# Layer 0's modulation as fp32 products on four 32-column tiles, and a pooling mixer with channels on partitions

## The chip, the cores and the metric

The kernel runs on one core of a Trainium2 chip. The metric is device time: three runs took 1964.33, 1965.14 and 1966.70 us, median 1965.14 us. Work is spread over TensorE (matmuls and transposes into PSUM), VectorE, ScalarE, GpSimd, and DMA transfers issued from SyncE. In the rows PE is TensorE, PEld its weight loads, DVE VectorE, ACT ScalarE, POOL GpSimd, SP SyncE.

## The reference

A two-layer decoder trunk on 256 tokens of width 2048, batch one, fp32. Layer 0 mixes tokens by causal pooling, layer 1 by latent attention (which the change leaves alone); both have a SwiGLU FFN of width 5632. Each sub-layer is modulated by a conditioning vector `c`. What matters here:

```python
sc = jax.nn.silu(c)
shift_m, scale_m, gate_m, shift_f, scale_f, gate_f = jnp.split(sc @ mod_w[i] + mod_b[i], 6, axis=-1)
h = modulate(rmsnorm(x, norm_mix[i]), shift_m, scale_m)       # h * (1 + scale) + shift
y = pool_mixer(h, pool_w[i], pool_scale[i])                   # layer 0
x = x + gate_m[:, None, :] * y
h = modulate(rmsnorm(x, norm_ffn[i]), shift_f, scale_f)
x = x + gate_f[:, None, :] * swiglu(h, ffn_gate[i], ffn_up[i], ffn_down[i])
```

`pool_mixer` takes, in four groups of 512 channels, the causal mean over 2, 4, 8 or 16 tokens less the value itself, multiplies each group by a 512x512 matrix and scales the channels by `pool_scale`. `mod_w[0]` alone is 2048 x 12288 fp32, 100 MB; a sixth of it (2048 x 2048, a "part") is 16.8 MB.

## The kernel before

Weights arrive as units of 1 MiB (128 x 2048 fp32, or 512 x 512) in a ring of six buffers, `raw`. For the large projections each unit is split exactly into two fp32r halves (ScalarE copies the upper half, L368, VectorE subtracts it, L370) and multiplied in three combinations: 24 matmuls of 512 columns a unit (L392). The program calls everything ahead of the first of these the front; it makes layer 0's mixer and the first quarter of the FFN's hidden state.

The modulation of the front is four groups of units: shift (16 units), scale (16), gate (16) and the first 512 columns of the FFN's shift and scale ("block 0", 8 units). In `Part.add` (L183) VectorE multiplies a unit by 128 values of silu(c), one for each partition, and adds it to an accumulator 128 x 2048; at the end TensorE sums over partitions with a vector of ones (L275). For the gate, `SharedPart` gives five of the 16 row tiles to TensorE as fp32 matmuls with the value of c repeated over 128 columns (L200), and adds VectorE's accumulator the same way (L199). Block 0 (`BlockPart`, L219 to L247) is divided too: seven row tiles by TensorE with one column of weights (L230), nine by VectorE (L233).

The mixer holds tokens on partitions at its ends and channels on partitions in the middle: band matrices times the normed stream (L726, L727), scale and shift per channel (L797 on ScalarE, L799 on VectorE), the 512x512 products (L784) with tokens on partitions again, `pool_scale` (L791), the gate and the residual add (L525, L526), squares for the norm (L410), and for each quarter of the hidden state a scaling by token (L432 or L434), eight transposes (L444) and the modulation (L458 to L460).

Two things set the order. Inside `tc.manual_schedule()` instructions stand as they are written; elsewhere a scheduler orders each engine's queue by priority. `pump(n)` emits the next n units of a list of background work, which is how gate and block 0 are interleaved with the mixer here, and blocks 1 to 3 of the FFN's shift and scale with the start of the FFN. In that start (`start_ffn`), twelve projections go through quarter after quarter of the hidden state, and the next quarter's scaling, transposes and modulation are emitted between units. The residual stream `x` is written aside to DRAM at the FFN's fifth chunk (`stream_aside`).

## Time and profile before

| | us |
|---|---|
| median of three runs | 1965.14 |
| span of the profiled execution, first to last instruction | 1962.3 |
| TensorE, first fp32r product of the FFN starts at | 184.32 |
| TensorE busy after 184 us, of 1778.3 | 1751.0 |
| TensorE busy in the whole span | 1853.0 |
| VectorE busy in the whole span | 1546.4 |

The profile lists one execution of 1962.3 us; the 2.8 us up to the median lie outside its first and last instruction. Up to 184 us the DMA engines move weights for the front and TensorE works in bursts; from there on TensorE is busy nearly without a break. A busy share is that of a stretch, so the front has to be read by itself.

### The profile page before, as it was taken

What the parts mean: (1) busy time and instruction counts of PE and PEld (TensorE: products, weight loads), DVE (VectorE), ACT (ScalarE), POOL (GpSimd) and SP (SyncE); (2) the same over time, 40 slices, a digit from 0 to 9 for tenths busy, and PEclk for the clock granted to TensorE, in tenths of its full rate; (3) what the DMA queues carried; (4) which work ended last, traced back from release to release, by engine and by line L of the source; (5) the groups of instructions that cost most, each with busy time, mean ns of one, the idle gap of its engine ahead of it and who ended that gap; (6) DMA issues with size and microseconds to landing.
All of it is one profiled execution on the core that took longest, in us unless ns stands there. A gap on an engine that the chain in (4) does not pass through costs nothing. (4 is left out here: it accounts for less than half of the span.)

```text
span 1962.3 us, 21516 instructions
## 1 busy us (share of the span) xinstructions
PE 1853.0 (94%) x8485; PEld 1520.7 (77%) x8485; DVE 1546.4 (79%) x1312; ACT 850.0 (43%) x939; POOL 35.9 (2%) x33
## 2 busy tenths in 40 slices
...
GB/s 377 408 378 365 379 321 305 310 350 327 313 329 302 332 325 345 338 333 284 307 311 304 228 295 142 360 303 325 297 293 260 225 229 257 235 209 186 195 219 70
DMA packets 225184, 572.66 MB, mean 292 GB/s; under 512 B 11958, under 2 KB 16286, under 8 KB 203442
## 3 DMA queue, kind: packets, MB, share of 16 engines
...
## 5 line engine op out<-in xcount | busy, mean ns | idle before, releaser
L392 PE MATMUL ps<-hl,act 128*128 128x512 f32 x7008 | 1609.5, 391 | 4.7 <-ACT act L459 2.2
L392 PEld LDWEIGHTS ps<-hl,act 128*128 128x128 f32 x7008 | 1315.1, 188 | 279.3 <-ACT act L459 4.4
L370 DVE TENSOR_TENSOR hl<-raw,hl 128x2048 fp32r<-128x2048 f32 x296 | 676.2, 2289 | 239.9 <-ACT hl L368 236.1
L368 ACT ACTIVATE hl<-raw 128x2048 fp32r<-128x2048 f32 x296 | 566.4, 1919 | 608.7 <-PE ps L392 542.1
L183 DVE SCALAR_TENSOR_TENSOR acc<-raw,s_col,acc 128x2048 f32<-128x2048 f32 x155 | 364.0, 2348 | 4.2 <-DMA raw<-in_mod_w_dram 1.6
L233 DVE SCALAR_TENSOR_TENSOR acc<-raw,s_col,acc 128x1024 f32<-128x1024 f32 x121 | 155.0, 1281 | 8.7 <-DMA raw<-in_mod_w_dram 7.2
L556 DVE TENSOR_TENSOR act<-ps,act 128x512 f32<-128x512 f32 x96 | 64.6, 687 | 14.1 <-PE ps L392 13.7
L275 PE MATMUL ps<-ones,acc 128*128 128x1 f32 x64 | 13.9, 352 | 62.8 <-DVE acc L183 39.9
L410 ACT ACTIVATE junk<-x 128x512 bf16<-128x512 f32 x40 | 25.2, 630 | 89.6 <-DVE x L526 44.1
L275 PEld LDWEIGHTS ps<-ones,acc 128*128 128x128 f32 x64 | 13.8, 332 | 64.5 <-DVE acc L183 41.4
L590 ACT ACTIVATE act<-ps 128x512 fp32r<-128x512 f32 x44 | 23.8, 596 | 61.5 <-PE ps L587 53.4
L625 DVE TENSOR_TENSOR x<-ps,x 128x512 f32<-128x512 f32 x32 | 22.1, 691 | 35.4 <-PE ps L392 35.4
L458 ACT ACTIVATE t2k<-ps,cols 128x256 f32<-128x256 f32 x64 | 33.2, 567 | 21.6 <-PE ps L444 17.0
L634 ACT ACTIVATE t2k<-ps 128x512 f32<-128x512 f32 x24 | 14.2, 593 | 64.2 <-PE ps L392 64.2
L918 PE MATMUL ps<-act,hl 128*128 128x256 f32 x128 | 37.2, 291 | 0.6 <-DVE hl L370 0.6
L919 PE MATMUL ps<-act,hl 128*128 128x256 f32 x128 | 36.7, 287 | 0.0
L920 PE MATMUL ps<-act,hl 128*128 128x256 f32 x128 | 36.1, 286 | 0.0
L591 DVE TENSOR_TENSOR act<-ps,act 128x512 fp32r<-128x512 f32 x44 | 28.2, 685 | 8.1 <-ACT act L590 8.0
L638 DVE TENSOR_TENSOR t2k<-ps,t2k 128x512 f32<-128x512 f32 x24 | 16.6, 690 | 21.3 <-PE ps L392 21.3
L444 PE MATMUL ps<-con,t2k 128*128 128x128 f32 x144 | 22.5, 306 | 11.2 <-DVE t2k L432 8.1
L784 PE MATMUL ps<-act,act 128*128 128x512 f32 x64 | 30.7, 644 | 0.9 <-issue 0.9
L554 ACT ACTIVATE act<-ps 128x512 f32<-128x512 f32 x32 | 19.1, 598 | 28.3 <-PE ps L392 28.1
...
## 6 DMA issues: line engine op xcount, KB each, us to landing
raw<-in_mod_w_dram SPq DMA_DIRECT2D x128, 1024.0 KB
...
raw<-in_mod_w_dram SPq DMA_DIRECT2D x128, 512.0 KB
...
```

What stands on the lines that cost most here:

```text
L183: dve.scalar_tensor_tensor(out=self.acc, in0=r, scalar=s_col[:, self.kt:self.kt + 1], in1=self.acc, op0=ALU.mult, op1=ALU.add)
L233: dve.scalar_tensor_tensor(out=self.acc, in0=r[:, k], scalar=s_, in1=self.acc, op0=ALU.mult, op1=ALU.add)
L368: hi_ins = act.activation(hi, r, AF.Copy)
L370: lo_ins = dve.tensor_tensor(out=lo, in0=r, in1=hi.bitcast(F32), op=ALU.subtract)
L392: pe.matmul(banks[tok], lhsT=t_[:, i, k, tok * P:(tok + 1) * P], rhs=w[:, k, :], start=first and n < len(part), stop=last and n >= len(ord ...
L458: act.activation(full, pts[k // 2][:, k % 2, :], AF.Identity, scale=scale, bias=bias)
L556: dve.tensor_tensor(out=part, in0=banks[tok], in1=part, op=ALU.add)
L591: dve.tensor_tensor(out=m[:, 1, :, ts_], in0=v, in1=m[:, 0, :, ts_].bitcast(F32), op=ALU.subtract)
L784: pe.matmul(pt, lhsT=pooled[g // 2][:, g % 2, k, tok * P:(tok + 1) * P], rhs=wp[g][:, k, :], start=k == 0, stop=k == KL - 1)
L918: pe.matmul(pt[:, h, :], lhsT=wl(h0 + h, k), rhs=t_[:, 0, k, :], start=k == 0, stop=False)
L919: pe.matmul(pt[:, h, :], lhsT=wh(h0 + h, k), rhs=t_[:, 0, k, :], start=False, stop=False)
L920: pe.matmul(pt[:, h, :], lhsT=wh(h0 + h, k), rhs=t_[:, 1, k, :], start=False, stop=k == KL - 1)
```

## The change

The layer 0 modulation leaves VectorE. A class `Strips` takes every unit of shift, scale, gate and block 0. The unit's 2048 columns are four strips of 512; each is an fp32 matmul of its own whose weights are 32 columns wide (silu(c) in the first, zeros in the others), and the four write rows 0, 32, 64 and 96 of one PSUM bank. The built program gives them the tile size 128 x 32 and the tile positions 0, 32, 64 and 96. After 16 units (8 for block 0) ScalarE copies the bank, and four small matmuls with a selecting matrix turn the four rows into columns with channels on partitions, to which VectorE adds the bias.

The mixer keeps channels on partitions to its end. The residual stream is transposed at the start (`xT`, which takes the memory of `x`), products give channels by tokens, and gate, pool scale and residual add are one VectorE instruction for each 128 channels. The sum of squares is taken by TensorE (32 matmuls of one column). The reciprocal root, one value for each token, is spread over partitions: a diagonal matrix times ones. The hidden state needs one multiplication with that row and no transposes. The stream is transposed back for the copy in DRAM, which is now written while the FFN's start is in its second quarter.

All of the front stands in a fixed order, given by a table: after unit n of the 56, these functions. The first five units and both halves of x are requested at once.

```diff
+    crow = t2k([KD, P])
+    vrows = t2k([V_END, P])
+    brows = t2k([5 * KD, P])
+
+    def load_x(tok):
+        sync.dma_start(xn[tok], a["x"][0, tok * P:(tok + 1) * P, :])
...
+    def load_ahead():
+        kt = len(ahead)
+        ahead.append(raw_t([P, 1, NSTRIP, CH]))
+        sync.dma_start(ahead[kt].rearrange("p k i n -> p (k i n)"), a["mod_w"][0, kt * P:(kt + 1) * P, :D])
...
+    load_x(0)
+    sync.dma_start(crow, a["c"].rearrange("b (r q) -> (b r) q", q=P))
+    sync.dma_start(con, a["con"])
+    load_ahead()
+    load_rows(V_NM, "norm_mix", "l (r q) -> (l r) q")
+    load_ahead()
...
+    front = work.tile([P, KD * (STRIP + 7)], F32, tag="acc", bufs=2, name="front")
+    s_strip = front[:, :KD * STRIP].rearrange("p (k m) -> p k m", m=STRIP)
+    bcol = front[:, KD * STRIP:KD * (STRIP + 5)].rearrange("p (i k) -> p i k", k=KD)
+    gm_col, ps_col = (front[:, KD * (STRIP + i):KD * (STRIP + i + 1)] for i in (5, 6))
+    pool.memset(front[:, :KD * STRIP], 0.0)
...
+    dve.tensor_copy(s_strip[:, :, 0], s_col)
...
-    # a gate on all partitions, with some of its row tiles summed on the idle tensor engine
-    class SharedPart(Part):
-        def add(self, r):
+    class Strips:
+        def __init__(self, i, pair, done):
+            self.n, self.rows, self.done, self.kt = (2, 2, done, 0) if pair else (NSTRIP, 1, done, 0)
+            w = a["mod_w"][0][:, i * D:(i + self.rows) * D]
...
+        def use(self, r):
             if self.kt == 0:
-                self.banks = [ps_t() for _ in range(ND)]
-            if self.kt not in GM_PE:
-                super().add(r)
-                return
-            rep = t2k([P, P])
-            act.activation(rep, ones, AF.Copy, scale=s_col[:, self.kt:self.kt + 1])
-            for j in range(ND):
-                js = slice(j * CH, (j + 1) * CH)
-                if self.kt == KD - 1:
-                    pe.matmul(self.banks[j], lhsT=ones, rhs=self.acc[:, js], start=False, stop=False)
-                pe.matmul(self.banks[j], lhsT=rep, rhs=r[:, js], start=self.kt == GM_PE[0], stop=self.kt == KD - 1)
-
-    # the same for CH columns of shift and scale at once, two row tiles in a unit
+                self.bank = ps_t()
+            for m in range(NSTRIP):
+                k, i = m // self.n, m % self.n
+                pe.matmul(self.bank[m * STRIP:(m + 1) * STRIP, :], lhsT=s_strip[:, self.kt + k, :], rhs=r[:, k, i, :],
+                          start=self.kt == 0, stop=self.kt + self.rows == KD)
+            self.kt += self.rows
+            if self.kt == KD:
+                self.done(self.columns())
...
+        def columns(self):
+
+            rows = t2k([P, CH])
+            act.activation(rows, self.bank, AF.Copy)
+            pick = con[:, C_SEL:C_SEL + NSTRIP] if self.rows == 1 else con[:, C_PAIR:C_PAIR + 2]
+            pt = ps_t()
+            for b in range(KL):
+                pe.matmul(pt[:, b * self.n:(b + 1) * self.n], lhsT=rows[:, b * P:(b + 1) * P], rhs=pick, start=True,
+                          stop=True)
...
-    def start_ffn(l, rstd, first, cshift, cscale, late):
+    def start_ffn(l, first, ahead, hidden, late):
...
             for j in range(ND - 1):
+                if l == 0 and j == 1:
+                    for tok in range(NT):
+                        sync.dma_start(aside[0][:, tok], back[tok])
                 todo = KD // 2 if j + 1 >= ND - late else 0
                 for n, (c, which) in enumerate((c, w) for c in begun for w in (GATE, UP)):
                     if n == 2 * len(begun) - 1:
-                        hT.append(modulated(turned_pieces(pieces), j + 1, cscale, cshift))
+                        hT.append(hidden(j + 1, pieces))
...
-    cs = slice(2 * D, 3 * D)
-    gm = SharedPart(a["mod_w"][0][:, cs], a["mod_b"][0:1, cs], lambda acc: None)
-    push(gm)
-    for j in range(ND):
-        push(sf_block(0, j, C_SF0, C_AF0, j == 0), KD // 2)
...
+    shift = Strips(0, False, lambda v: with_bias(cols[:, C_SM0, :], v, 0))
+    scale = Strips(1, False, lambda v: with_bias(cols[:, C_AM0, :], v, 1, vcol[:, V_NM:V_NM + KD]))
+    gate = Strips(2, False, lambda v: with_bias(gm_col, v, 2, ps_col))
+    block = Strips(3, True, block_cols)
...
+        pt = ps_t().rearrange("p (k t) -> p k t", k=2)
+        for i in range(2):
+            ks = slice((2 * h2 + i) * P, (2 * h2 + i + 1) * P)
+            pe.matmul(pt[:, i, :], lhsT=norm[g][0][:, ks], rhs=band[:, g, :T], start=True, stop=False)
+            pe.matmul(pt[:, i, P:T], lhsT=norm[g][1][:, ks], rhs=band[:, g, T:], start=False, stop=True)
+        act.activation(pool_all[g // 2][:, g % 2, 2 * h2:2 * h2 + 2, :], pt, AF.Copy)
...
+    def pool_modulate(g):
+        for k in range(KL):
+            kt = g * KL + k
+            sh = t2k([P, T])
+            act.activation(sh, flat_all[:, g, :], AF.Copy, scale=cols[:, C_SM0, kt:kt + 1])
+            d_ = pool_all[g // 2][:, g % 2, k, :]
+            dve.scalar_tensor_tensor(out=d_, in0=d_, scalar=cols[:, C_AM0, kt:kt + 1], in1=sh, op0=ALU.mult, op1=ALU.add)
...
+    def pool_product(g, n):
...
+        ns = slice(n * P, (n + 1) * P)
+        for k in range(KL):
+            pe.matmul(mixed[g][:, n % 2, :], lhsT=wp[g][:, k, ns], rhs=pool_all[g // 2][:, g % 2, k, :],
+                      start=k == 0, stop=k == KL - 1)
+        if n % 2 == 1:
+            act.activation(ysum[g // 2][:, g % 2, n - 1:n + 1, :], mixed[g], AF.Copy)
...
+    def mix_in(g):
+
+        for k in range(KL):
+            kt = g * KL + k
+            dve.scalar_tensor_tensor(out=xT[:, kt, :], in0=ysum[g // 2][:, g % 2, k, :], scalar=gm_col[:, kt:kt + 1],
+                                     in1=xT[:, kt, :], op0=ALU.mult, op1=ALU.add)
...
+        for h2 in range(2):
+            sq = t2k([P, 2, T])
+            act.activation(sq, xT[:, g * KL + 2 * h2:g * KL + 2 * h2 + 2, :], AF.Square)
+            squares[g].append(sq)
+
+    def mix_total(g):
+        for k in range(KL):
+            for tok in range(NT):
+                pe.matmul(total[:, tok:tok + 1], lhsT=squares[g][k // 2][:, k % 2, tok * P:(tok + 1) * P], rhs=ones[:, 0:1],
+                          start=g + k + tok == 0, stop=g == ND - 1 and k == KL - 1 and tok == NT - 1)
...
+    def turn_back(g):
         for tok in range(NT):
             pt = ps_t()
             for k in range(KL):
-                pe.matmul(pt, lhsT=pooled[g // 2][:, g % 2, k, tok * P:(tok + 1) * P], rhs=wp[g][:, k, :],
-                          start=k == 0, stop=k == KL - 1)
-            act.activation(y[tok][:, g * CH:(g + 1) * CH], pt, AF.Copy)
...
+                pe.transpose(pt[:, k * P:(k + 1) * P], xT[:, g * KL + k, tok * P:(tok + 1) * P], ident)
+            dve.tensor_copy(back[tok][:, g * CH:(g + 1) * CH], pt)
...
+    def norm_total():
+
+        r = small([P, NT])
+        rsqrt_mean(r, total[:, :NT], D)
+        diag = t2k([P, NT, P])
         for tok in range(NT):
-            dve.tensor_tensor(out=y[tok][:, gs], in0=y[tok][:, gs], in1=psc[:, gs], op=ALU.mult)
+            dve.tensor_scalar(out=diag[:, tok, :], in0=ident, scalar1=r[:, tok:tok + 1], scalar2=None, op0=ALU.mult)
+        pt = ps_t()
+        pe.matmul(pt[:, :T], lhsT=ones, rhs=diag.rearrange("p t q -> p (t q)"), start=True, stop=True)
+        act.activation(rstd_b, pt[:, :T], AF.Copy)
...
+    def hidden_T(j):
+        parts = []
+        for k in range(KL):
+            if k % 2 == 0:
+                both = t2k([P, 2, T])
+            dve.tensor_tensor(out=both[:, k % 2, :], in0=xT[:, j * KL + k, :], in1=rstd_b, op=ALU.mult)
+            parts.append(both[:, k % 2, :])
+        return parts
+
+    def halves_T(j, parts):
+        t_ = act_t([P, 2, KL, T])
+        for k, full in enumerate(parts):
+            kt = j * KL + k
+            scale, bias = (cols[:, i, kt:kt + 1] for i in (C_AF0, C_SF0))
+            act.activation(full, full, AF.Identity, scale=scale, bias=bias)
+            act.activation(t_[:, 0, k, :], full, AF.Copy)
+            mod_ins[0] = dve.tensor_tensor(out=t_[:, 1, k, :], in0=full, in1=t_[:, 0, k, :].bitcast(F32),
+                                           op=ALU.subtract)
+        return t_
...
+    units = [shift] * KD + [scale] * KD + [gate] * KD + [block] * (KD // 2)
+    n_mix, n_block = 2 * KD, 3 * KD
...
+    for g in range(ND):
+        then(n_mix - 8 + 2 * g, load_pool_w, g)
+        then(n_mix - 1 + g, pool_modulate, g)
+        for q in range(4):
+            then(n_mix + 4 * g + q, pool_product, g, q)
+        then(n_block - 1, mix_in, g)
+        then(n_block + g, mix_total, g)
+        then(n_block + 3 + g, turn_back, g)
+    then(n_block + 3, norm_total)
+    then(n_block + 4, lambda: first.append(hidden_T(0)))
+    then(n_block + 5, lambda: w_early(ffn_weights(0)[GATE][0:CH, 0:CH]))
...
     with tc.manual_schedule():
-        for kt in range(KD):
-            g, k = kt // KL, kt % KL
-            sh = t2k([P, T])
-            act.activation(sh, flat[:, g, :], AF.Copy, scale=cols[:, C_SM0, kt:kt + 1])
-            d_ = pooled[g // 2][:, g % 2, k, :]
-            dve.scalar_tensor_tensor(out=d_, in0=d_, scalar=cols[:, C_AM0, kt:kt + 1], in1=sh, op0=ALU.mult, op1=ALU.add)
-        for g in range(ND):
-            pool_product(g)
-        pump(10)
-        for g in range(ND):
-            pool_scaled(g)
-            if g % 2:
-                pump(2)
-        pump(2)
...
+        for n, part in enumerate(units):
+            if n < len(ahead):
+                part.use(ahead[n])
+            else:
+                part.unit()
+            for f, args in after.get(n, ()):
+                f(*args)
+        first = halves_T(0, first[0])
...
-        first = modulated(pts, 0, C_AF0, C_SF0)
```

What this does to the queues is seen in three places. The first is TensorE's queue at the pooling products; L784 and L200 are the old products and the gate's row tiles.

```order
L784 MATMUL ps_468<-act_388,act_234 128x512 x4
L784 MATMUL ps_474<-act_388,act_234 128x512 x4
L784 MATMUL ps_480<-act_390,act_234 128x512 x4
L784 MATMUL ps_486<-act_390,act_234 128x512 x4
L200 MATMUL ps_497<-raw_523,t2k_525 128x512
L200 MATMUL ps_498<-raw_523,t2k_525 128x512
L200 MATMUL ps_499<-raw_523,t2k_525 128x512
L200 MATMUL ps_500<-raw_523,t2k_525 128x512
```

In the changed kernel L260 is a group of four strips, L273 the four small matmuls that give the columns, and L845 the new pooling products.

```order
L273 MATMUL ps_511<-con,t2k_509 128x4 x4
L260 MATMUL ps_532<-raw_530,front 32x512 x4
L845 MATMUL ps_537<-act_118,act_459 128x256 x4
L260 MATMUL ps_532<-raw_554,front 32x512 x4
L845 MATMUL ps_537<-act_118,act_459 128x256 x4
L260 MATMUL ps_532<-raw_577,front 32x512 x4
L845 MATMUL ps_583<-act_118,act_459 128x256 x4
L260 MATMUL ps_532<-raw_600,front 32x512 x4
L845 MATMUL ps_583<-act_118,act_459 128x256 x4
```

Products that stood in one run ahead of the gate's units now alternate with them, four of 256 columns after each unit.

The second is TensorE's queue at the end of the front. Before, the last transposes of the first quarter (L444) and the sums of block 0 over partitions (L247) stand there, right ahead of the first FFN products (L392).

```order
L444 MATMUL ps_687<-con,t2k_668 128x128
L444 MATMUL ps_687<-con,t2k_666 128x128
L444 MATMUL ps_687<-con,t2k_668 128x128
L247 MATMUL ps_695<-ones,t2k_696 128x1 x4
L247 MATMUL ps_695<-ones,t2k_702 128x1 x4
L247 MATMUL ps_695<-ones,acc_585 128x1 x8
L392 MATMUL ps_749<-hl_722,act_726 128x512
L392 MATMUL ps_750<-hl_722,act_726 128x512
```

After it, L867 is the sum of squares, L875 the transposes back, L886 the spread of the norm.

```order
L875 MATMUL ps_837<-con,x 128x128 x4
L875 MATMUL ps_843<-con,x 128x128 x4
L867 MATMUL ps_114<-ones,t2k_780 128x1 x4
L867 MATMUL ps_114<-ones,t2k_782 128x1 x4
L886 MATMUL ps_864<-t2k_861,ones 128x256
L260 MATMUL ps_787<-raw_867,front 32x512 x4
L875 MATMUL ps_874<-con,x 128x128 x4
L875 MATMUL ps_880<-con,x 128x128 x4
L260 MATMUL ps_787<-raw_892,front 32x512 x4
L875 MATMUL ps_899<-con,x 128x128 x4
L875 MATMUL ps_905<-con,x 128x128 x4
L260 MATMUL ps_787<-raw_917,front 32x512 x4
```

The block's eight units now have the sum of squares, the spread and the transposes back between them, all on TensorE.

The third is VectorE's queue at the start of the FFN. Before, L460 is the lower half of the hidden state, L233 the background's accumulation, L370 the split of a unit.

```order
L460 TENSOR_TENSOR act_726<-t2k_727,act_726 128x256
L460 TENSOR_TENSOR act_726<-t2k_731,act_726 128x256
L460 TENSOR_TENSOR act_726<-t2k_735,act_726 128x256
L460 TENSOR_TENSOR act_726<-t2k_739,act_726 128x256
L233 SCALAR_TENSOR_TENSOR acc_775<-raw_778,s_col,acc_775 128x1024 x2
L233 SCALAR_TENSOR_TENSOR acc_775<-raw_815,s_col,acc_775 128x1024
L370 TENSOR_TENSOR hl_788<-raw_785,hl_787 128x2048
L233 SCALAR_TENSOR_TENSOR acc_775<-raw_815,s_col,acc_775 128x1024
L233 SCALAR_TENSOR_TENSOR acc_775<-raw_852,s_col,acc_775 128x1024
L370 TENSOR_TENSOR hl_825<-raw_822,hl_824 128x2048
```

In the changed kernel these are L905, L293 and L411, and L894 is the multiplication of the stream by the norm's row.

```order
L905 TENSOR_TENSOR act_953<-t2k_886,act_953 128x256 x2
L905 TENSOR_TENSOR act_953<-t2k_889,act_953 128x256 x2
L293 SCALAR_TENSOR_TENSOR acc_999<-raw_1002,s_col,acc_999 128x1024
L894 TENSOR_TENSOR t2k_1271<-x,krT 128x256
L293 SCALAR_TENSOR_TENSOR acc_999<-raw_1002,s_col,acc_999 128x1024
L894 TENSOR_TENSOR t2k_1271<-x,krT 128x256
L894 TENSOR_TENSOR t2k_1274<-x,krT 128x256 x2
L894 TENSOR_TENSOR t2k_1748<-x,krT 128x256 x2
L293 SCALAR_TENSOR_TENSOR acc_999<-raw_1039,s_col,acc_999 128x1024
L411 TENSOR_TENSOR hl_1012<-raw_1009,hl_1011 128x2048
L293 SCALAR_TENSOR_TENSOR acc_999<-raw_1039,s_col,acc_999 128x1024
L894 TENSOR_TENSOR t2k_1751<-x,krT 128x256 x2
```

The multiplications for the later three quarters (twelve of 128 x 256) stand in the queue between the first accumulations and the first splits.

## Rows read from the trace of the kernel before

**Rows 1.** The page, span and instructions.

```profile
span 1962.3 us, 21516 instructions
```

**Rows 2.** Windows: stretch, length, busy us (instructions) per engine, clock, DMA share, GB/s.

```profile
20.00:57.00 37.00, 0.37 (x2) 0.37 (x2) 34.59 (x15) 3.59 (x7) 0.00 (x0) 1.00 1.01 421
...
82.00:116.00 34.00, 13.07 (x40) 9.46 (x41) 26.52 (x27) 3.76 (x9) 0.95 (x1) 0.50 1.02 410
...
145.00:152.00 7.00, 7.00 (x18) 3.07 (x17) 1.42 (x1) 0.00 (x0) 0.00 (x0) 1.00 0.72 237
152.00:181.00 29.00, 26.66 (x85) 10.36 (x84) 22.67 (x29) 8.88 (x19) 1.65 (x2) 1.00 1.04 378
...
188.00:260.00 72.00, 72.00 (x324) 59.70 (x323) 65.97 (x52) 43.30 (x46) 0.95 (x1) 1.00 1.01 366
260.00:340.00 80.00, 80.00 (x359) 66.34 (x358) 73.13 (x71) 31.08 (x24) 1.81 (x1) 1.00 0.88 305
```

**Rows 3.** Timeline, VectorE: start, us, instruction, count, wait before it.

```profile
19.31 14.81 DVE L183 SCALAR_TENSOR_TENSOR acc<-raw,s_col,acc 128x2048 f32<-128x2048 f32 x6 [0.16 <-DMA raw<-in_mod_w_dram]
34.27 12.32 DVE L183 SCALAR_TENSOR_TENSOR acc<-raw,s_col,acc 128x2048 f32<-128x2048 f32 x5 [0.15 <-DMA raw<-in_mod_w_dram]
```

**Rows 4.** Timeline, ScalarE, 3 to 6 us.

```profile
5.65 0.63 ACT L410 ACTIVATE junk<-x 128x512 bf16<-128x512 f32 x1 [3.31 <-DMA x<-in_x_dram]
```

**Rows 5.** Waits of the DMA queue, first 200 us: total, times, longest.

```profile
SPq L219 <- PE ps L200: 10.7, 4, 5.6
```

**Rows 6.** Timeline, TensorE; each fp32 matmul leaves two records.

```profile
14.22 2.55 PE L702 MATMUL ps<-t2k,ones 1*128 1x512 f32 x8 [6.20 <-DMA t2k<-in_pool_scale_dram]
56.63 6.99 PE L275 MATMUL ps<-ones,acc 128*128 128x1 f32 x32 [39.86 <-DVE acc L183]
...
109.89 30.70 PE L784 MATMUL ps<-act,act 128*128 128x512 f32 x64 [0.90 <-issue]
...
162.36 12.18 PE L230 MATMUL ps<-raw,s_col 128*1 128x512 f32 x28
174.47 1.36 PE L444 MATMUL ps<-con,t2k 128*128 128x128 f32 x8
175.75 1.94 PE L247 MATMUL ps<-ones,t2k 1*128 1x1 f32 x16
180.00 2.90 PE L247 MATMUL ps<-ones,acc 128*128 128x1 f32 x16 [2.30 <-DVE acc L233]
184.32 3.03 PE L392 MATMUL ps<-hl,act 128*128 128x512 f32 x6 [1.43 <-ACT act L459]
```

**Rows 7.** Source line L702: count, duration ns min/median/max, first and last start.

```profile
L702 PE MATMUL ps<-t2k,ones x8: 1052/1120/1217, 14.2 to 15.7; 1*128 1x512 f32 x8
```

**Rows 8.** Source line L230, same columns.

```profile
L230 PEld LDWEIGHTS ps<-raw,s_col x28: 79/84/84, 162.4 to 173.5; 128*1 128x1 f32 x28
L230 PE MATMUL ps<-raw,s_col x28: 590/593/593, 162.4 to 173.9; 128*1 128x512 f32 x28
```

**Rows 9.** Groups by line, 0 to 188 us: busy us, mean ns, idle before.

```profile
L797 ACT ACTIVATE t2k<-hl,cols 128x256 f32<-128x256 f32 x16 | 7.3, 501 | 31.0 <-DVE act L799 29.5 <-PE ps L726 1.5
...
L799 DVE SCALAR_TENSOR_TENSOR act<-act,cols,t2k 128x256 f32<-128x256 f32 x16 | 6.4, 477 | 0.1
...
L786 ACT ACTIVATE act<-ps 128x512 f32<-128x512 f32 x8 | 4.8, 598 | 22.9 <-PE ps L784 22.9
...
L415 POOL TENSOR_TENSOR rstd<-sm,mhalf 128x2 f32<-128x2 f32 x2 | 1.4, 702 | 22.2 <-DVE sm L414 11.6 <-DMA raw<-in_mod_w_dram 10.6
```

**Rows 10.** The page, costliest groups, VectorE.

```profile
L370 DVE TENSOR_TENSOR hl<-raw,hl 128x2048 fp32r<-128x2048 f32 x296 | 676.2, 2289 | 239.9 <-ACT hl L368 236.1
...
L233 DVE SCALAR_TENSOR_TENSOR acc<-raw,s_col,acc 128x1024 f32<-128x1024 f32 x121 | 155.0, 1281 | 8.7 <-DMA raw<-in_mod_w_dram 7.2
```

**Rows 11.** Chain of waits, longest pieces: start, us, what.

```profile
1346.25 0.87 PE ps L444 x8
1347.12 59.85 PE ps L392 x264
```

252 lines of the change are left out of this document (128 added, 124 removed).

## The prediction

> **What bounds the kernel now.** I read the windows first, since the program has two halves with different limits. From 188 us on TensorE is busy 72.00 of 72 and 80.00 of 80 us [rows 2]: an edit there counts only if it takes time off TensorE or makes it wait. Ahead of that, between 20 and 57 us, TensorE is busy 0.37 of 37 us while the DMA engines are full at 421 GB/s [rows 2]. The change lies in this front, so the question is when the first FFN product can start, 184.32 us now [rows 6].
>
> What paces the front is seen on VectorE's timeline: six accumulations start 19.31 to 34.27 us, each group ending in a short wait for a weight transfer [rows 3], so a unit of 1 MiB lands every (34.27 - 19.31)/6 = 2.49 us and VectorE just keeps up. Later that pace is lost. Between 145 and 152 us the DMA rate drops to 237 GB/s while TensorE is busy throughout [rows 2], and the DMA queue waits 10.7 us for the gate's products on TensorE (L200) to free buffers [rows 5]. The end of the front before is therefore set by TensorE and VectorE in turn, not by DMA. Until 116 us TensorE also ran at half clock, 1.2 of 2.4 GHz, the granted clock being 0.50 from 82 to 116 us [rows 2], with hardly a product ahead of the pooling products at 109.89 us [rows 6].
>
> **The change part by part.** All sums are made against the profiled span of 1962.3 us [rows 1]; the median is 2.8 us above it. I follow TensorE's new queue, because every unit of the front now passes it.
>
> *Units 0 to 31 (shift, scale).* The first half of x lands at 5.65 us [rows 4]; after it come 38.2 MiB to the end of unit 31 (32 units, four pool matrices now requested ahead of the gate, the other half of x, band 0.75, constants and tables 0.4). At 2.49 us each unit 31 lands at 100.9 us. TensorE has time here: a group of strips must only stay under 2.49 us on average, with six buffers to absorb the band products. So VectorE's 32 accumulations go at no gain; DMA is the cover, and it is gone once TensorE is slower than the units land.
>
> *A group of strips.* No row shows four 32-column tiles at once. One such tile alone does: L230, 28 records or 14 fp32 matmuls of 512 columns, took 12.18 us [rows 6], 0.87 us each. So four cost 0.87 us if they run entirely side by side and 3.48 us if in turn. The nearest row is L702, four matmuls on the four 32-row tiles: eight records of about 1.12 us [rows 7], 9.0 us of work, were over in 2.55 us [rows 6]. They did run side by side. A record there lasts twice the 0.59 us of L230 [rows 8], which fits half clock, so at full clock the four would take 1.28 us. I take 1.1: 0.87 for one tile's two records and three weight loads of 0.08 [rows 8] by which the others start later. A change of tile size adds little: L230's records step by (12.18 - 0.59)/27 = 0.429 us; L444 starts 174.47 - 162.36 = 12.11 us after the first of them, 0.1 more than 28 steps. I take 0.1 per change. With strips standing between full-size products that is 1.2 us a unit; bounds 0.87 and 3.7.
>
> The Trainium skill (TensorEngine Tiling (Array Packing), Key Properties) says that changing the tiling mode drains TensorE. L444 began 0.07 us before L230's last record ended [rows 6], so in this trace the pipeline did not empty. By the rule each change would cost the tail of a record, 0.59 - 0.43 = 0.16 us, and the sum below would be 48 x 0.06 = 3 us later.
>
> For column tiles only the skill has a price (TensorE: Matmul & The Clock Gate, Measured speedup vs the span model): three column tiles ran 2.38 times as fast as in turn. By it four strips would take about 1.26 x 0.87 = 1.1 us, an estimate from that page; no run here shows it.
>
> *Gate, units 32 to 47.* The first pooling product waits for scale's columns: strips 1.1, ScalarE's copy 0.60 (as L786), four shift rows on ScalarE at 7.3/16 = 0.46, and the last VectorE step 0.48 [rows 9]: 100.9 + 1.1 + 0.6 + 1.8 + 0.5 = 104.9 us. The products are the old work in other shape: L784, 32 matmuls of 512 columns in 30.70 us, 6.1 us of it at half clock, is 27.6 us at full clock or 0.86 each [rows 2, 6]; four of 256 columns are 1.73 us. A unit thus takes TensorE 1.2 + 1.73 = 2.93 us against 2.49 for its transfer: **from here TensorE is the bound**. Fifteen strips and fifteen products bring it to 104.9 + 44.0 = 148.9 us; the gate's columns cost 0.6 + 1.0 (four small matmuls at 0.24, as L247 by 1.94/8 [rows 6]) and the last product 1.7: 152.2 us. VectorE's 16 gated adds, 0.4 to 0.48 each, run beside the next strips.
>
> *Block 0, units 48 to 55.* On TensorE: eight strips 9.6; 32 matmuls of the squares with one column; 32 transposes back; the spread of the norm. The column sums are bounded by L247 at 0.24 and L275 at 6.99/16 = 0.44 us each [rows 6]; the first ran at full clock (1.00 from 152 to 181 us [rows 2]), as these will, so 7.7 us (14.0 at the other end). Eight transposes take 0.87 us net in a full stream [rows 11]: 3.5. The norm makes TensorE wait for the GpSimd power, 0.70 [rows 9], and three short steps, 1.9 together by my estimate. Sum 22.7, so 174.9 us; then the copy and small matmuls 1.6, and columns to first product 1.4, as 182.90 to 184.32 us before [rows 6]. **The FFN starts at 177.9 us, 6.4 earlier.**
>
> *The FFN's start.* Three quarters lose their eight transposes: 3 x 0.87 = 2.6 us off a full TensorE. VectorE gets twelve multiplications of about 0.4 us, and they stand early. After the first quarter's subtractions the queue held three accumulations of 1.28 and a split of 2.29 [rows 10]; now six multiplications as well, 2.5 us. TensorE takes 59.85/11 = 5.44 us a unit [rows 11]; the split it waits for had 1.3 us to spare (done 6.2 us after the accumulations begin, needed 7.5 us after), now it is 1.2 late. The next is 2.6 + 2.1 + 2.3 = 7.0 us behind it against 5.44, 1.5 late; the third is on time. That gives back 2.7 us. ScalarE's two scalings per quarter fall away, at nothing, since TensorE hides them. The copy to DRAM moves from chunk five to the second quarter, 2 MiB or 5 us of transfer; between 260 and 340 us the DMA share is 0.88, 9.6 us free [rows 2], so nothing, or up to 5.
>
> *Clock.* Strips alone keep TensorE under half busy between 45 and 101 us; should the clock have fallen, the gate's first products run at half speed for about the 6.1 us seen before, at 3 us. I put 1.0.
>
> Sum: -6.4 - 2.6 + 2.7 + 1.0 = -5.3 us; 1957.0 in the span, 1960 as the median.
>
> **The rivals.** *The strips run in turn.* L230 speaks for it only as far as one tile goes, L702 against it, though there the tiles were rows and the moving operand one partition each; four strips read 128 partitions each. Price: 24 groups at 3.7 instead of 1.2 are 60 us from unit 32 on; before that 32 x 3.5 = 112 us from 8 us make unit 31 done at 120 or later instead of 102. At least 1960 + 60 + 18 = 2038 us. It decides from 2.5 us a group, where even the first half outruns its transfers; the change is slower already from about 1.45 a group.
>
> *Half side by side.* If a tile's second record holds back the next tile's first, four strips take five steps of 0.43 us, 2.15, with the change of size 2.35: 24 x 1.15 = 28 us, 1988. L702's starts, all eight within 1.5 us [rows 7], speak against it.
>
> *DMA paces the whole front.* If strips, sums and switches cost TensorE less, the last unit lands 63.2 MiB after x, at 163.2 us, and the FFN starts 1.1 + 3.0 later, at 167.3: 17.0 earlier, and 1965.1 - 17.0 - 2.6 + 2.7 = 1948. It needs about 11 us off the 73 us that TensorE takes from 104.9; the floor of 0.87 a group is worth 7.9.
>
> *The start is earlier and nothing comes of it.* From 188 to 260 us the DMA share is 1.01 [rows 2]; if transfers, not TensorE, set that stretch, an earlier start only waits for them: about 1965. Against it, TensorE is busy without a gap there.
>
> **How the numbers follow.** 0.2%, or 3.9 us, is about what a measurement can tell from no change. My forecast, four tiles side by side and TensorE the bound, 62%: its own range is 1949 (0.87 a group, no late splits) to 1973 (1.48 a group, the column sums at 0.44), with 41% faster, 12% same, 9% slower. DMA-paced 12%, faster. Nothing comes of it 7%, same. Half side by side 10%, in turn 9%, both slower. Together faster 53%, same 19%, slower 28%. The range 1947 to 1990 leaves out the strips in turn and little else.
>
> **What would show it.** Strips right: four L260 matmuls (eight records) in about 1.1 us between 60 and 100 us, and units still landing at 2.49 us. TensorE as the bound: no gaps from 105 to 175 us, the DMA queue waiting for TensorE there. The column sums: L867 at 0.24 us. The late splits: two short waits of the FFN's products (L433 in the changed kernel) for a split (L411) at the start. The first L433 at 178 us. The forecast is wrong if a group takes over 1.4 us, if TensorE waits for transfers in the gate, or if the time from first product to the end differs from before by more than 3 us.

## The result and the profile after

The changed kernel took 1971.29 us (median of 7 executions, 1970.22 to 1972.76) against 1965.48 us for the kernel before on the same chip (7 executions, 1964.33 to 1966.7). The ratio is 1.0032, 95% interval 1.0022 to 1.0043: slower by 0.3%, where 1960 us, 0.3% faster, was forecast. The profiled execution is the longest of the seven (1972.76 us), so its span lies 8.7 us above that of [rows 1] where the medians differ by 5.8:

```profile
span 1971.0 us, 22348 instructions
```

The windows of the changed kernel have the columns of [rows 2]: stretch, length, busy time and instructions of TensorE, its weight loads, VectorE, ScalarE and GpSimd, then the granted clock, the DMA share and GB/s. They show TensorE full from 260 to 340 us, as before. What differs lies ahead of it.

```profile
80.00:101.00 21.00, 11.61 (x48) 1.22 (x48) 0.00 (x0) 0.00 (x0) 0.00 (x0) 0.51 1.02 405
...
160.00:165.00 5.00, 5.00 (x46) 3.50 (x38) 4.55 (x13) 4.16 (x7) 0.00 (x0) 1.00 0.79 241
165.00:170.00 5.00, 5.00 (x27) 3.35 (x26) 0.31 (x1) 0.63 (x1) 0.00 (x0) 0.55 0.94 309
170.00:175.00 5.00, 5.00 (x24) 3.33 (x25) 1.13 (x2) 0.00 (x0) 0.00 (x0) 0.50 0.61 195
175.00:180.00 5.00, 3.36 (x15) 3.14 (x15) 0.89 (x4) 0.00 (x0) 0.70 (x1) 0.50 0.42 160
180.00:185.00 5.00, 5.00 (x31) 1.84 (x30) 1.85 (x4) 2.18 (x2) 0.00 (x0) 0.74 0.19 46
...
260.00:340.00 80.00, 80.00 (x356) 66.24 (x355) 74.98 (x70) 33.10 (x25) 1.81 (x1) 1.00 0.93 328
```

The eighth column is the granted clock. It is 0.51, 1.2 of 2.4 GHz, in the stretch with strips alone (80 to 101 us), and again 0.50 to 0.55 from 165 to 180 us. From 160 to 175 us TensorE is busy 5.00 of 5.00 us three times over: no idle time lies in the 5 us ahead of that second fall.

TensorE's timeline of the changed kernel answers [rows 6]. L260 is a group of four strips, L273 the small matmuls that pick columns, L845 a pooling product (four matmuls), L867 eight of the one-column sums, L886 the diagonal's product, L433 the FFN. A "unit of the gate" below is one group of strips and the pooling product behind it.

```profile
104.05 1.93 PE L260 MATMUL ps<-raw,front 128*32 128x512 f32 x8 [3.23 <-DMA raw<-in_mod_w_dram]
...
110.36 3.78 PE L845 MATMUL ps<-act,act 128*128 128x256 f32 x8
...
117.09 1.07 PE L260 MATMUL ps<-raw,front 128*32 128x512 f32 x8
118.08 1.99 PE L845 MATMUL ps<-act,act 128*128 128x256 f32 x8
120.01 1.07 PE L260 MATMUL ps<-raw,front 128*32 128x512 f32 x8
...
160.65 1.95 PE L867 MATMUL ps<-ones,t2k 128*128 128x1 f32 x16
...
165.39 1.86 PE L260 MATMUL ps<-raw,front 128*32 128x512 f32 x8
167.18 3.58 PE L867 MATMUL ps<-ones,t2k 128*128 128x1 f32 x16
...
174.31 3.41 PE L867 MATMUL ps<-ones,t2k 128*128 128x1 f32 x16
179.37 1.19 PE L886 MATMUL ps<-t2k,ones 128*128 128x256 f32 x2 [1.64 <-DVE t2k L884]
...
192.01 0.73 PE L433 MATMUL ps<-hl,act 128*128 128x512 f32 x2 [1.60 <-ACT act L904]
```

Three things are to be seen. At full clock a unit of the gate takes 120.01 - 117.09 = 2.92 us, as forecast. At half clock these instructions take nearly twice as long: strips 1.93 for 1.07, the first product 3.78 for 1.99, eight sums 3.4 to 3.6 for 1.95. And the first FFN product starts at 192.01 us, 7.7 later than the 184.32 before and 14.1 later than the forecast 177.9. From there to the end it is 1779.0 us, against 1778.0 before: 7.7 of the 8.7 us between the two spans are lost in the front.

The 14.1 us, by the forecast's own steps (measured less forecast): unit 31's strips at 104.05 for 100.9, **+3.15**; from there to the first pooling product 6.31 for 4.0, **+2.3**; from that to the end of the last product, 159.65 - 110.36 = 49.3 for 47.3, **+2.0**; from that to the first FFN product 32.4 for 25.7, **+6.7**.

### The profile page after: what moved, and what is told of

The parts are those of the page before. It is cut to its first block, busy times and chain, and to the rows that moved or that the text cites. A ratio compares the mean times of both kernels' runs of the same rounds, so it can differ in the third digit from the quotient of the medians.

```text
span 1971.0 us, 22348 instructions
## 1 busy us (share of the span) xinstructions
PE 1895.6 (96%) x8949; PEld 1532.0 (78%) x8949; DVE 1442.2 (73%) x1298; ACT 843.0 (43%) x915; POOL 30.1 (2%) x30
## 5 line engine op out<-in xcount | busy, mean ns | idle before, releaser
L433 PE MATMUL ps<-hl,act 128*128 128x512 f32 x7008 | 1610.9, 391 | 6.2 <-ACT hl L409 2.7
L433 PEld LDWEIGHTS ps<-hl,act 128*128 128x128 f32 x7008 | 1317.1, 189 | 282.1 <-ACT hl L409 3.6
L411 DVE TENSOR_TENSOR hl<-raw,hl 128x2048 fp32r<-128x2048 f32 x296 | 676.3, 2288 | 244.1 <-ACT hl L409 239.8
L409 ACT ACTIVATE hl<-raw 128x2048 fp32r<-128x2048 f32 x296 | 566.5, 1917 | 666.3 <-PE ps L433 595.0
L235 DVE SCALAR_TENSOR_TENSOR acc<-raw,s_col,acc 128x2048 f32<-128x2048 f32 x112 | 262.6, 2345 | 1.2 <-DMA raw<-in_mod_w_dram 1.0
L293 DVE SCALAR_TENSOR_TENSOR acc<-raw,s_col,acc 128x1024 f32<-128x1024 f32 x112 | 143.3, 1279 | 2.1 <-DMA raw<-in_mod_w_dram 0.8
L260 PE MATMUL ps<-raw,front 128*32 128x512 f32 x448 | 74.0, 749 | 26.3 <-DMA raw<-in_mod_w_dram 26.2
L260 PEld LDWEIGHTS ps<-raw,front 128*32 128x32 f32 x448 | 10.4, 121 | 61.2 <-DMA raw<-in_mod_w_dram 46.3
L452 ACT ACTIVATE junk<-x 128x512 bf16<-128x512 f32 x24 | 15.1, 628 | 59.9 <-DVE x L550 39.7
L845 PEld LDWEIGHTS ps<-act,act 128*128 128x128 f32 x128 | 24.1, 198 | 16.3 <-issue 12.6
L783 DVE TENSOR_TENSOR cols<-ps,front 128x16 f32<-128x16 f32 (+1 forms) x4 | 0.6, 166 | 49.3 <-PE ps L273 49.2
L682 DVE TENSOR_TENSOR t2k<-ps,t2k 128x512 f32<-128x512 f32 x24 | 16.6, 690 | 25.7 <-PE ps L433 25.7
L845 PE MATMUL ps<-act,act 128*128 128x256 f32 x128 | 33.7, 408 | 0.0
L500 ACT ACTIVATE t2k<-ps,cols 128x256 f32<-128x256 f32 x48 | 24.8, 569 | 12.4 <-PE ps L486 11.8
```

Source lines behind the costliest of these rows:

```text
L235: dve.scalar_tensor_tensor(out=self.acc, in0=r, scalar=s_col[:, self.kt:self.kt + 1], in1=self.acc, op0=ALU.mult, op1=ALU.add)
L260: pe.matmul(self.bank[m * STRIP:(m + 1) * STRIP, :], lhsT=s_strip[:, self.kt + k, :], rhs=r[:, k, i, :], start=self.kt == 0, stop=self.kt ...
L293: dve.scalar_tensor_tensor(out=self.acc, in0=r[:, k], scalar=s_col[:, self.kt + k:self.kt + k + 1], in1=self.acc, op0=ALU.mult, op1=ALU.add)
L409: hi_ins = act.activation(hi, r, AF.Copy)
L411: lo_ins = dve.tensor_tensor(out=lo, in0=r, in1=hi.bitcast(F32), op=ALU.subtract)
L433: pe.matmul(banks[tok], lhsT=t_[:, i, k, tok * P:(tok + 1) * P], rhs=w[:, k, :], start=first and n < len(part), stop=last and n >= len(ord ...
```

## The experiments

The theory, T1, is that the clock was mis-sized: it falls where the one-column sums run (first half), and where strips alone, or a wait for transfers, go before the gate (second half). Its rivals are R1, the last stage is long by its work and order, whatever the clock; R2, TensorE's work in the gate, or the landing of unit 31, sets the pace, whatever the clock; and R3, an earlier FFN start brings nothing. Later T2 was added: transfers asked for too early hold up unit 31. In the code cuts, `...` stands for what is left out. Times are medians, each beside the kernel before on the same chip at 1965.3 to 1965.8 us.

### sum64: the sums over 64 columns

```diff
-  pe.matmul(total[:, tok:tok + 1], lhsT=squares..., rhs=ones[:, 0:1], ...)
+  pe.matmul(total[:, tok * 64:tok * 64 + 64], lhsT=squares..., rhs=ones[:, 0:64], ...)
...
-  rsqrt_mean(r, total[:, :NT], D)
+  rsqrt_mean(r, total[:, :2 * 64]...[:, :, 0], D)
```

> The changed kernel with one edit: each of the 32 column sums of the norm multiplies by 64 columns of ones where it multiplied by one, and the norm takes the first of the 64. The products, their weights, their order and the values read are the same; TensorE only moves more columns. Theory T1 (what was mis-sized is the clock of the stage of FFN block 0: the granted clock fell to 0.50 from 165.5 to 182.6 us of the span of the changed kernel, just after the one-column sums began, and eight sums then took 3.4 to 3.6 us where they take 1.95): the clock stays at its upper level or falls much later, the groups of sums stay near 2 to 2.5 us, and the first product of the FFN comes 4 to 7 us earlier than at 192.0: about 1965 to 1967 us. Rival R1 (the stage is long because of its work and its order, whatever the clock): the added columns make it longer, 1971 to 1975. Rival R3 (what the front gains is lost later): the first FFN product earlier, the time within 1 us of 1971.

Measured 1965.38 us, ratio 1.0001 (0.9992 to 1.0010), so 5.9 us less than the changed kernel. Its TensorE timeline and its windows of the same stretch:

```profile
166.71 2.00 PE L867 MATMUL ps<-ones,t2k 128*128 128x64 f32 x16
...
170.56 1.90 PE L867 MATMUL ps<-ones,t2k 128*128 128x64 f32 x16
...
185.25 0.73 PE L433 MATMUL ps<-hl,act 128*128 128x512 f32 x2 [1.60 <-ACT act L904]
```

```profile
165.00:170.00 5.00, 5.00 (x42) 3.19 (x42) 0.52 (x2) 0.76 (x2) 0.00 (x0) 1.00 1.02 359
170.00:175.00 5.00, 3.35 (x29) 2.77 (x31) 1.93 (x5) 0.19 (x1) 0.70 (x1) 1.00 0.88 312
```

The clock stays at 1.00 and the FFN starts 6.8 us earlier. Eight sums over 64 columns take 2.00 us where eight over one column took 1.95 at full clock: the added columns are nearly free. (Each sum loads 128 x 128 weights in either form, which may be why; no run separates it.) The first half of T1 holds; R1 and R3 fall.

### spread and fill: TensorE kept at work beside the strips

Run spread: `then(6 + i, pool_half, ...)` becomes `then(6 + 3 * i, pool_half, ...)`. Run fill adds one product to each of the units 14 to 30:

```diff
+  def filler(n):
+      pt = ps_t()
+      pe.matmul(pt, lhsT=ident, rhs=xn[n % 2][:, :CH], start=True, stop=True)
...
+  for i in range(14, n_mix - 1):
+      then(i, filler, i)
```

> The changed kernel with one edit: the eight halves of the pooling (transposes and band products on TensorE) stand behind units 6, 9, 12 to 27 of weights, where they stood behind units 6 to 13. Nothing is added or taken away. T1 (TensorE, which had 1.07 us of strips in each 2.49 us from 70 to 101 us, was at half clock there, and went into the gate's units at half clock, where the first product took 3.78 us against 1.99): the clock of that stretch rises or at least the gate begins at the upper level, the first product of the FFN comes 2 to 4 us earlier, 1967 to 1969 us. R2 (the gate's units are bound by TensorE's work after a start that the landing of unit 31 sets, whatever the clock): within 1 us of 1971.

> The changed kernel with work added: behind each of the units 14 to 30 of weights, where TensorE has the strips alone, one more product of 128 x 512 whose result nobody reads (17 of them, about 0.87 us each at the upper clock, beside transfers of 2.49 us a unit). T1: TensorE no longer falls to half clock there, the gate's first product starts and runs at the upper clock, and the time falls by 2 to 4 us, to 1967 to 1969, although work was added. R2 and R1: nothing is gained, 1971 to 1972; if the added products hold up the strips, and so the buffers, up to 1976.

Measured: spread 1971.95 us, ratio 1.0029 (1.0018 to 1.0040); fill 1970.63 us, ratio 1.0025 (1.0016 to 1.0034). No gain that can be measured beside the changed kernel, as R2 expected; T1's 1967 to 1969 us was missed. The windows and the timeline of fill show why:

```profile
96.00:100.00 4.00, 3.11 (x18) 0.61 (x18) 0.00 (x0) 0.00 (x0) 0.00 (x0) 1.00 1.01 391
100.00:104.00 4.00, 1.13 (x6) 0.30 (x2) 0.00 (x0) 0.00 (x0) 0.00 (x0) 0.90 1.04 428
104.00:108.00 4.00, 3.13 (x14) 1.40 (x14) 0.00 (x0) 1.85 (x5) 0.00 (x0) 0.50 1.01 418
```

```profile
104.15 1.93 PE L260 MATMUL ps<-raw,front 128*32 128x512 f32 x8 [3.02 <-DMA raw<-in_mod_w_dram]
...
110.47 3.43 PE L849 MATMUL ps<-act,act 128*128 128x256 f32 x8
```

The clock was up from 96 to 100 us and fell all the same around the 3.02 us wait for unit 31, so the gate still began at half clock. Unit 31's strips came at 104.15 us, as in the changed kernel (104.05): at half clock or not, the stretch of strips alone costs nothing, since transfers set the pace there.

### wide: the norm's sums by all-ones weights

```diff
-  for tok in range(NT):
-      pe.matmul(total[:, tok:tok + 1], lhsT=squares..., rhs=ones[:, 0:1], ...)
+  pe.matmul(total[:, :T], lhsT=ones, rhs=squares[g][k // 2][:, k % 2, :], ...)
...
-  rsqrt_mean(r, total[:, :NT], D)
...
-  act.activation(rstd_b, pt[:, :T], AF.Copy)
...
+  pool.tensor_tensor(out=rstd_b, in0=v[:, 0, :], in1=v[:, 1, :], op=ALU.pow)
```

> The changed kernel with the norm's sums in another shape: instead of 32 products with one column of ones, each with its own 128 x 128 weights, 16 products of all-ones weights with 256 columns of squares, which leave the sum of each token on all partitions; so the diagonal, its product and its copy go, and the power is taken of 128 x 256 by GpSimd. TensorE's time for the sums at the upper clock is about the same (16 x 0.43 = 7 us against 7.8). T1: no fall of the clock in this stage, 4 to 7 us less in it, and up to 2 us less or more for the chain from the sums to the first modulated block, which the wide power on GpSimd may lengthen: 1963 to 1968. R1 (the work and order of the stage): only the chain changes, 1969 to 1973. R3: the first FFN product earlier, the time within 1 us of 1971.

Measured 1999.96 us, ratio 1.0175 (1.0162 to 1.0189), outside every expectation. GpSimd's timeline tells the reason, and its windows what the sums did:

```profile
172.71 41.25 POOL L882 TENSOR_TENSOR krT<-t2k 128x256 f32<-128x256 f32 x1 [9.73 <-DVE t2k L881]
```

```profile
165.00:170.00 5.00, 5.00 (x33) 2.50 (x33) 0.21 (x2) 2.47 (x2) 0.00 (x0) 1.00 1.01 353
```

The sums now stand on all partitions, so the power is taken of 128 x 256 values. The power of 256 elements per partition took 41.25 us, 0.16 us an element, where two elements take 0.70 [rows 9]. The clock stayed at 1.00 through these sums too. As a whole the run says nothing on R1.

### head, poolw and both: the gate's beginning

All three have the sums of sum64. Head moves the pooling halves so that the last two fill the wait for unit 31; poolw asks for three of the four pool matrices among the gate's units; both does the two.

```diff
 head
-  for i in range(2 * ND): then(6 + i, pool_half, i // 2, i % 2)
+  for i, n in enumerate((9, 12, 15, 18, 21, 24, 30, 30)): then(n, pool_half, i // 2, i % 2)
 poolw
-  then(n_mix - 8 + 2 * g, load_pool_w, g)
+  then(n_mix - 2 + 4 * g, load_pool_w, g)
```

> The kernel with sums over 64 columns (run sum64, 1965.4 us), and the halves of the pooling behind units 9, 12, 15, 18, 21, 24, 30 and 30 in place of 6 to 13: the last two now fill the stretch from 100 to 104 us in which TensorE waited for unit 31 (the run fill, which kept TensorE at work up to 101 us, still went into the gate at half clock after that wait of 3.0 us). T1 (the gate begins slowly because the clock has fallen): the first product of the gate takes 2.0 us in place of 3.78, and it starts near 108 in place of 110.3; the first product of the FFN comes 3 to 4.5 us earlier than at 185.25: 1961 to 1962.5 us. Rival (the landing of unit 31 and the chain behind it set the gate, whatever the clock, or the added halves hold it up): 1965 to 1967.

> The kernel with sums over 64 columns (1965.4 us), and the four pool matrices of 1 MiB each requested behind units 30, 34, 38 and 42 in place of 24, 26, 28 and 30. The bytes and the products are the same. Theory T2 (the gate's units are bound by TensorE at 2.92 us against some 2.55 us for a transfer, so their transfers have time to spare, while ahead of unit 31 transfers are the bound): unit 31 lands 7 to 10 us earlier, near 95 to 97 us; the gate starts earlier by as much and then takes its transfers' pace of about 2.6 us for 1 MiB, 19 MiB long; the first product of the FFN 4 to 7 us earlier than at 185.25: 1959 to 1962. Rival (the bytes of the whole front set its end): nothing gained in the gate, 1964 to 1966.

> The two edits together, halves behind units 9 to 24 and 30, and the pool matrices behind units 30 to 42, with the sums over 64 columns. If the clock at the head and the place of the pool matrices are two separate costs, their gains add until transfers bind the whole gate: 1956 to 1960. If either takes the other's gain (the wait for unit 31 shorter in any case, so nothing left for the clock), the better of the two alone, within 1 us of it. Rival (neither counts): 1965.

Measured: head 1963.15 us, ratio 0.9988 (0.9980 to 0.9997); poolw 1957.45 us, ratio 0.9961 (0.9949 to 0.9974); both 1955.89 us, ratio 0.9952 (0.9939 to 0.9964). TensorE's timeline of poolw, then of both:

```profile
96.50 1.94 PE L260 MATMUL ps<-raw,front 128*32 128x512 f32 x8 [3.24 <-DMA raw<-in_mod_w_dram]
...
102.81 2.73 PE L845 MATMUL ps<-act,act 128*128 128x256 f32 x8
...
165.80 1.93 PE L260 MATMUL ps<-raw,front 128*32 128x512 f32 x8
167.66 1.82 PE L875 MATMUL ps<-con,x 128*128 128x128 f32 x8
...
177.96 0.73 PE L433 MATMUL ps<-hl,act 128*128 128x512 f32 x2 [1.60 <-ACT act L904]
```

```profile
96.15 1.07 PE L260 MATMUL ps<-raw,front 128*32 128x512 f32 x8
...
100.17 1.96 PE L845 MATMUL ps<-act,act 128*128 128x256 f32 x8
...
175.19 0.73 PE L433 MATMUL ps<-hl,act 128*128 128x512 f32 x2 [1.60 <-ACT act L904]
```

Poolw: unit 31's strips start at 96.50 us instead of 104.02 in sum64, and the FFN starts 7.3 us earlier (177.96 for 185.25). T2 holds: three transfers of 1 MiB stood ahead of a unit that TensorE waited for, and in the gate there was room for them; its units still take 2.92 us, without a wait for a transfer. The two rows from 165.80 us show that the sums over 64 columns don't keep the clock up in every case: it fell to half there, behind TensorE's 1.64 us wait for the norm's power, and this stage took 27.0 us for 25.4 in sum64.

Both: with the clock up, the way from unit 31's strips to the first product is 100.17 - 96.15 = 4.02 us, the forecast's 4.0, where at half clock it was 6.31 (poolw: 102.81 - 96.50). That is the clock's price at the head, and the product's own 0.8 us (1.96 for 2.73) comes to it. The wait for unit 31 is filled in both; in poolw it was 3.24 us. The FFN starts 2.8 us earlier than in poolw, but that is not the head's gain alone. Up to the gate's second strips both is 3.4 us ahead (102.06 for 105.48); in the gate it loses 2.25, as TensorE now waits 0.20, 0.92 and 0.93 us for transfers; and 1.6 come from the fall at 165.80 us, which both doesn't have. The medians differ by 1.6 us, with intervals that overlap, so the second half of T1 rests on the rows of the gate's beginning and not on the time. There the landing of unit 31, which R2 named, is the larger part (7.5 us, poolw) and the clock the smaller (3.1).

Head alone missed its 3 to 4.5 us. Its added halves began at half clock and held unit 31's strips up to 107.0 us. By then the clock was up (the strips took 1.06 us), but the gate's first product was slow all the same, though the wait was filled; why isn't shown:

```profile
111.06 3.31 PE L845 MATMUL ps<-act,act 128*128 128x256 f32 x8 [0.17 <-PE ps L260]
```

The first FFN product came at 185.46. What head gained, 2 us by the medians, isn't in the front: about 1.0 us lies in the FFN's first 240 products (57.9 us for 58.9 in sum64), and the rest behind them isn't explained.

### share: six of the gate's units on VectorE

```diff
+  class SharedStrips(Strips):
+      def use(self, r):
+          if self.kt in (2, 4, 6, 8, 10, 12):
+              dve.scalar_tensor_tensor(out=self.acc, in0=r[:, 0], scalar=s_col[...], in1=self.acc, ...)
+              self.kt += 1
+              return
+          if self.kt == KD - 2:
+              for m in range(NSTRIP):
+                  pe.matmul(self.bank[...], lhsT=o_strip, rhs=self.acc[:, m, :], ...)
```

> The kernel with sums over 64 columns (1965.4 us), and six of the gate's sixteen units (the 3rd, 5th, 7th, 9th, 11th, 13th) summed by VectorE, which is idle there, into a tile that TensorE adds with one more group of strips. TensorE loses five groups of strips, about 1.0 us each. Theory (TensorE is the bound in the gate at 2.92 us a unit): the gate ends 3 to 5 us earlier, 1960.5 to 1962.5. Rival (the gate is bound by its transfers, or by its slow start alone): within 1 us of 1965.4; if VectorE's accumulations hold up the scaled shifts before the products, up to 1968.

In `o_strip` the first of 32 columns is ones. Measured 1958.35 us, ratio 0.9964 (0.9951 to 0.9978), 7.0 us less than sum64. TensorE's timeline (L263 strips, L865 products, L453 the FFN):

```profile
114.00 1.07 PE L263 MATMUL ps<-raw,front 128*32 128x512 f32 x8
115.00 3.72 PE L865 MATMUL ps<-act,act 128*128 128x256 f32 x16
118.65 1.07 PE L263 MATMUL ps<-raw,front 128*32 128x512 f32 x8
...
153.18 1.06 PE L263 MATMUL ps<-raw,front 128*32 128x512 f32 x8
...
180.14 48.96 PE L453 MATMUL ps<-hl,act 128*128 128x512 f32 x200 [1.60 <-ACT act L924]
```

Two units take 118.65 - 114.00 = 4.65 us in place of 5.84. The block's first strips, behind the gate, start 6.7 us earlier (153.18 for 159.86): TensorE did bound the gate. The FFN starts only 5.1 us earlier, since the clock fell behind the wait for the norm's power here too, and the stage took 27.0 us for 25.4. The other 2 us of the time came after the FFN's start.

### both1: the one-column sums back in both

> The kernel of run both (1955.9 us) with the one-column sums of the changed kernel back in place of those over 64 columns. T1 (the one-column sums themselves let the clock fall): half clock again some us after the first of them, eight sums at 3.4 to 3.6 us in place of 2.0, and 4 to 7 us lost: 1960 to 1963. Rival (the fall in the changed kernel came from the half clock at the gate's head or the time of the stage, both changed here): the clock stays up, within 1 us of 1955.9.

The edit is that of sum64, reversed. Measured 1960.89 us, ratio 0.9971 (0.9961 to 0.9982), 5.0 more than both (4.6 when each is taken beside its own kernel before). The executions ran from 1957.0 to 1965.3 us; the profiled one was the longest. Its timeline and windows:

```profile
102.84 3.44 PE L845 MATMUL ps<-act,act 128*128 128x256 f32 x8
...
157.59 1.81 PE L260 MATMUL ps<-raw,front 128*32 128x512 f32 x8
159.33 3.57 PE L867 MATMUL ps<-ones,t2k 128*128 128x1 f32 x16
...
184.21 0.73 PE L433 MATMUL ps<-hl,act 128*128 128x512 f32 x2 [1.60 <-ACT act L904]
```

```profile
160.00:165.00 5.00, 5.00 (x24) 3.32 (x25) 0.00 (x0) 0.00 (x0) 0.00 (x0) 0.50 1.05 385
```

The stage comes 8 us earlier in the span here, and the fall came again, 5 us after the first sum (157.6 after 152.84; in the changed kernel 165.4 after 160.65). From the end of the last product to the first FFN product it is 32.3 us, against 32.4 in the changed kernel and 25.4 with 64 columns. So the place in time is not the cause; the form of the sums is. In this execution the gate's first product, too, took 3.44 us where the profile of both has 1.96, at the same order of work and with the wait filled in each: whether the clock falls there differs from execution to execution. Only one execution's rows are there to read, and they don't explain the spread of 8 us. The three shortest, 1957.0 to 1958.0 us, lie within 2.1 us of the median of both, which leaves little room for the 6.9 us that the sums cost in the profiled one. Yet the mean granted clock of all eight, 0.981 to 0.986, is below that of both, 0.987 to 0.990. Whether the sums lost the clock in each of them stays open.

### gps, sum64gps and all: what is left

Gps (on both) and sum64gps (on sum64) put the twelve multiplications by the norm of quarters 1 to 3 on GpSimd: `(pool if j else dve).tensor_tensor(...)`. All is both with the edit of share.

> The kernel of run both (1955.9 us), with the twelve multiplications of quarters 1 to 3 by the norm, 128 x 256 each, on GpSimd in place of VectorE, where they stood between accumulations ahead of the splits that TensorE waits for. If late splits cost what the prediction said (2.7 us of the first FFN products) and are still there: the first sixty products close up and the time from the first FFN product to the end, 1776.4 us in the profile of both, falls by 1 to 2.7: 1953 to 1955. Rival (the run both no longer waits for splits, its products running 46.4 us in one piece): within 1 us. If GpSimd takes more than 2 us for one multiplication, the quarters themselves come late and it is slower, 1957 or more.

> The kernel with sums over 64 columns (run sum64, 1965.4 us), and the twelve multiplications of quarters 1 to 3 on GpSimd (0.91 us each in run gps) in place of VectorE. Here the late splits are there: TensorE's first 240 records of the FFN took from 185.25 to 244.3 us, 59.05, against 56.5 before the change. If the multiplications between VectorE's accumulations are what makes the splits late, as the prediction had it at 2.7 us: no pause before the products that wait for the splits, the 240 records in 56 to 57.8 us, and 1963 to 1964 us. Rival (the start of the FFN is slow for another reason, its clock or its transfers): the 240 records stay at 58 to 59 us and the time within 1 us of 1965.4.

> The kernel of run both (1955.9 us), with six of the gate's units summed by VectorE as in run share, where that was worth 7.0 us (1965.4 to 1958.4). With the pool matrices requested among the gate's units, the gate moves 19 to 20 MiB and TensorE already waits for transfers a little (18.24 of 20 us busy from 120 to 140 us). Theory (from there transfers bind the gate): 0 to 2 us gained, 1954 to 1956. Rival (TensorE is the bound still, the gains add): 1949 to 1951.

Measured: gps 1955.06 us, ratio 0.9950 (0.9936 to 0.9963); sum64gps 1964.56 us, ratio 0.9995 (0.9986 to 1.0004); all 1954.48 us, ratio 0.9951 (0.9939 to 0.9964). The timeline of sum64gps:

```profile
186.22 47.70 PE L433 MATMUL ps<-hl,act 128*128 128x512 f32 x200 [2.85 <-ACT act L904]
234.13 9.40 PE L433 MATMUL ps<-hl,act 128*128 128x512 f32 x40 [0.21 <-DVE hl L411]
243.37 0.30 PE L310 MATMUL ps<-acc,con 128*128 128x32 f32 x2
```

The first 200 products run in one piece, where sum64 waits 0.48 us for a split at 202.61. From the first FFN product to L310 it is 57.2 us against 58.9 in sum64. So the multiplications on VectorE cost 1.8 us of the forecast 2.7 in this stretch. But the first product comes 1.0 us later (186.22 for 185.25), and in the time 0.8 is left, inside the uncertainty. A likely reason for the 1.0: the first quarter's four multiplications stayed on VectorE and took 0.85 us each (median) beside those on GpSimd, where they took 0.42 in sum64. In gps nothing that can be measured is gained. All fits the bound by transfers: share's 7.0 us shrink to 1.4, inside the intervals, and TensorE waits 6.5 us for transfers in the gate, up to 2.97 at a time. The best kernels, both, gps and all, agree within their intervals at 0.995 of the kernel before.

## Why the prediction was wrong, point by point

**The step that failed is the term "Clock", put at +1.0 us.** It was argued from idle stretches alone, for the gate's head. The column sums were priced from L247 at 0.24 us, as "the first ran at full clock (1.00 from 152 to 181 us [rows 2]), as these will". At full clock they did take 0.24 (1.95 for eight). But after the second eight of them the clock fell to 0.50 and stayed there until about 182 us. That is the +6.7 us of the last stage; with the sums over 64 columns the stage takes 25.4 us (159.86 to 185.25) against the forecast's 25.7, and the time falls by 5.9 us. This alone turns slower into no change.

The kernel before had a sign of it that the prediction passed over. In [rows 6] L247 stands twice: eight sums took 1.94 us from 175.75, but the next eight, with 128 rows of weights as in the new sums, took 2.90 from 180.00. The window there:

```profile
181.00:187.60 6.60, 5.02 (x16) 3.40 (x16) 3.64 (x7) 4.25 (x10) 0.95 (x1) 0.50 1.05 387
```

That clock, too, had fallen some 5 us after the first one-column sum, though with a wait of 2.30 us between, so before the change the sums can't be told from the wait.

**Clock at the head: right place, too small.** The prediction saw that the gate's first products might run at half speed, at 3 us, and put 1.0. In the changed kernel it cost 2.3 us up to the first product and 1.8 in it, 4.1 together.

**Unit 31: transfers were counted, at too high a rate.** 38.2 MiB at 2.49 us were to land by 100.9; the strips started at 104.05, which is (104.05 - 5.65)/38.2 = 2.58 us a MiB, 405 to 420 GB/s in the windows for the 421 of [rows 2]. The +3.15 us is a rate taken from a short stretch and spread over 95 us. The prediction listed "four pool matrices now requested ahead of the gate" and priced them only inside that sum. It didn't ask whether they had to go first: poolw, where three of them go later, takes 7.9 us less than sum64.

**Strips side by side: right.** The source view of L260 (records, duration ns min/median/max, first and last start):

```profile
L260 PE MATMUL ps<-raw,front x448: 592/617/1062, 9.4 to 188.0; 128*32 128x512 f32 x150
```

Eight records of 0.6 us take 1.07 us at full clock, forecast 1.1; both rivals of it fall. Between 80 and 101 us, at half clock, a group took 1.93, above the 1.4 that was to show the forecast wrong; transfers set the pace there, so that it cost nothing. One reading on the way to the 1.1 isn't borne out. L702's records of 1.12 us were put down to half clock, but the profile gives a granted clock of 1.00 for 14 to 17 us. It gives 1.00 for 57 to 64 us too, where L275 took 0.44 us a sum, as L867 did at 0.50 (3.41/8 = 0.43). So early in the trace durations and granted clock disagree, and no run here settles which is right. A change of tile size costs little: two products in a row take 3.65 us (share), 1.83 each, and one between strips 1.93, so 0.1 for the two changes of a unit, where the prediction took 0.1 each; its product was 0.1 too short, which made up for it. The drain that the Trainium skill states (TensorEngine Tiling (Array Packing), Key Properties) is not seen beyond that.

**TensorE the bound in the gate: right**, 2.92 us a unit for 2.93, no wait for a transfer in it, and in share, with fewer strips, it ends 6.7 us earlier. The DMA queue waits for TensorE, where it waited for L200 in [rows 5]. The first 200 us (total, times, longest), of which 42.7 us in 17 waits fall between 105 and 160 us:

```profile
SPq L249 <- PE ps L260: 98.4, 46, 4.8
```

The rival that transfers pace the whole front was off for this kernel, and for poolw too, whose gate has no wait for a transfer. It comes into sight in both (2.05 us of such waits in the gate) and in all (6.5 us).

**The FFN's start: about right.** The first block, from the first FFN product to the small product behind it (L310, 251.26 us; L261 before, 240.70), grew from 56.4 to 59.25 us, +2.9 for the forecast +2.7; from there to the first transposes of the products (415.26; 407.42 before) it shrank from 166.7 to 164.0, -2.7 for -2.6. The +2.9 is nearer to the forecast than its parts are. These products of the changed kernel show what they waited for:

```profile
209.37 29.54 PE L433 MATMUL ps<-hl,act 128*128 128x512 f32 x129 [0.67 <-DVE hl L411]
239.73 2.11 PE L433 MATMUL ps<-hl,act 128*128 128x512 f32 x8 [0.83 <-ACT hl L409]
242.06 9.36 PE L433 MATMUL ps<-hl,act 128*128 128x512 f32 x40 [0.22 <-DVE hl L411]
```

The two waits for a split (L411) came, but at 0.67 and 0.22 us for the forecast 1.2 and 1.5; 0.83 is for ScalarE's copy of the upper half (L409), which the forecast didn't have. With the multiplications off VectorE (sum64gps) the block is 1.8 us shorter than in sum64, and what makes up the remaining 0.8 over the kernel before stays open. The rival "nothing comes of it" falls: where the FFN started 6.8 and 7.3 us earlier, 5.9 and 7.9 came back in the time.

**The chances.** "Slower" stood at 28%: 19% on strips that don't run side by side, and 9% on the upper end of the forecast's own range, 1949 to 1973 us, with 1.48 us a group and the column sums at 0.44. The measured 1971.29 lies inside that range, but the way there was another: the groups took 1.07, and the 32 sums 10.9 us (1.95, 1.95, 3.58 and 3.41), 0.34 each. The mechanism that made it slower, a clock that falls in a stretch without idle time, was on no list.
